# Hybrid encoder block: state sums moved into the output product of the SSM stage, paired sums merged

## The chip, the cores and the metric

One Trainium2 chip, one of its cores. The metric is the device time of one execution in microseconds (us). Engines are named as in the profile: PE (TensorE, matrix products; PEld its weight loads), DVE (VectorE), ACT (ScalarE), POOL (GpSimd), SP (SyncE, which here only issues DMAs). Each engine runs its own list of instructions in order; semaphores tie them together.

## The reference, cut to what matters

The kernel computes one encoder block over 2048 positions plus 16 learned meta tokens: an RMS norm, an input projection, a convolution group and a state-space group side by side, an output projection, a feed-forward part, and a final norm. The change lies in the state-space group (SSM, 32 groups of 16 channels, 64 complex states, two directions):

```
dt = jnp.exp(log_dt)[:, None];  lam_bar = jnp.exp(lam * dt)
b_bar = ((lam_bar - 1.0) / lam)[..., None] * b_mat
bu = jnp.einsum('gph,blgh->blgp', b_bar, u)            # input into the states
_, states = lax.associative_scan(op, (lam_bar, bu))    # x[l] = lam_bar * x[l-1] + bu[l], complex
return jnp.einsum('ghp,blgp->blgh', c_mat, states).real
```

The forward and the backward direction are added, a skip term D*u is added, and a GELU and a gated unit follow. All arithmetic is fp32.

## The kernel before, in words

The sequence is cut into 16 interleaved parts, so that the scan has to run over 130 columns only, with a 16-step product in front of it and one behind. Two groups of the 32 form a *block*, b = 0 to 15. The states of both directions lie on the 128 partitions (64 each).

For each block there is a preparation, `ssm_prep(b)`, and a run, `ssm_run(b)`. The preparation loads the block's packed parameters (tile `pkb`, two buffers), and forms complex outer products with `outer` (three products and two sums each, into `k1` and the result): `pb` (transposed on PE as `tr_wb`, copied to `wb`) and `pc` (three buffers) on DVE, and the table of phasors `tab`, cosine and sine, on POOL. A small product `k` of `pc` and `bk` (L701, L706) is sent to DRAM by ACT and read back by SP as the matrix `mt`.

The run loads `u`, multiplies it on PE with `wb` (the product called `v` at L737, into one PSUM buffer, not to be confused with the other tile called `v`, which is the convolution group's projection at L158 to L160), and then, on DVE: `r1`, `r2` (the product turned by the table: times cosine, times sine), `zi` (two sums, one real, one imaginary), two scans `zo` (one for each direction, with real decays `rh`), `s1`, `s2` (turned back: times cosine, times sine) and `st` (two sums). PE then forms the output product `y`: for each of four pieces two matmuls of `mt` with `u` (L770) and two of `pc` with `st` (L773), all summed in PSUM. ACT copies it out and sends it to DRAM. `r1`, `r2`, `zi`, `rh`, `zo` have one buffer each; `s1` and `s2` reuse those of `r1` and `r2`.

The scheduler of the language puts the instructions of all engines into one fixed order each, by priorities and its own costs. It places into the gaps on PE the projections of the convolution group and of the later `u` parts (tiles `u`, `g`, `v` at L158 to L160, 128x512 matmuls in groups of three). They are called *fillers* here: they do not depend on the SSM blocks, and those that do not stand between the blocks stand behind the last one. After the blocks come the gated unit, the convolution, the output projection and the feed-forward part, whose order in the program is untouched by the change: on every engine the lists are the same from the gated unit on.

The loop that drives the blocks is the lower one in the code: run b, then prepare b + 3.

Of the kernel before, what the change touches and what calls it, by code (L numbers as in the profile page):

```python
# [18 lines left out]
P = 128  # L19
# [3 lines left out]
H = 16  # L23
# [14 lines left out]
def hymba_kernel(ctx, tc, x, meta, norm_mix_g, w_in, conv_w, conv_b, conv_ln_g, conv_ln_b,  # L38
# [123 lines left out]
    with ExitStack() as es2:  # L162
# [181 lines left out]
        with (tc.tile_pool(name="pp", bufs=1, reuse_waits="tile") as PP,  # L344
# [133 lines left out]
            def ssm_params():  # L478
# [111 lines left out]
                for v in (bb, cc, phb):  # L590
                    sub(v[:, 2], v[:, 1], v[:, 0])
                    add(v[:, 3], v[:, 0], v[:, 1])
# [40 lines left out]
        with (tc.tile_pool(name="pb", bufs=1, reuse_waits="tile") as PB,  # L633
# [14 lines left out]
            def ssm_prep(b):  # L648
# [11 lines left out]
                def outer(o_re, o_im, a, b4, la, lb, on=V):  # L660
# [9 lines left out]
                    tt(o_re, k1, o_re, ALU.subtract)  # L670
                    tt(o_im, k1, o_im, ALU.add)
# [9 lines left out]
                outer(pb[:, :, 0], pb[:, :, 1], lpv, bb, minor(H), major(16))  # L681
# [10 lines left out]
                outer(pc[:, :, 0], pc[:, :, 1], lpc, cc, major(H), minor(16))  # L692
# [24 lines left out]
                for g in range(2):  # L717
                    for half in range(2):
                        SP.dma_start(mt[:, g, half, :],
                                     dap(gdr[b], (g * H + half * 8) * 34 * H + H, [[34 * H, 8], [H, 16], [1, 256]]))  # L720

                tab = tb_([P, 2, 2, 10, 13], f"tab{b}", tag="tab", bufs=3)
                outer(tab[:, 0], tab[:, 1], pha, phb, major(13), minor(10), GP)
                prep[b] = (wb, pc, mt, tab)

            def ssm_run(b):
# [15 lines left out]
                sinb = tabf[:, 1].unsqueeze(2).broadcast_to([P, 2, 2, W])  # L742
# [4 lines left out]
                mul(r2, psv, sinb)  # L747
                add(zi[:, :, 0, :], r1[:, :, 0, :], r2[:, :, 1, :])
                sub(zi[:, :, 1, :], r1[:, :, 1, :], r2[:, :, 0, :])
# [9 lines left out]
                s1 = tb_([P, 2, 2, W], f"s1_{b}", tag="r1")[:, :, :, 0:P]  # L759
                s2 = tb_([P, 2, 2, W], f"s2_{b}", tag="r2")[:, :, :, 0:P]  # L760
                mul(s1, zv, cosb[:, :, :, 2:W])
                mul(s2, zv, sinb[:, :, :, 2:W])
                st = tb_([P, 2, 2, P], f"st{b}", tag="st", bufs=2)
                sub(st[:, :, 0, :], s1[:, :, 0, :], s2[:, :, 1, :])
                add(st[:, :, 1, :], s1[:, :, 1, :], s2[:, :, 0, :])
                py = ks_ps(f"y{b}", [P, 2, 2, P])
                for g in range(2):
                    for ht in range(2):
# [3 lines left out]
                        for ri in range(2):  # L772
                            T.matmul(py[:, g, ht, :],  # L773
                                     pc[:, g, ri, 8 * ht:8 * ht + 8, :].rearrange("p i h -> p (i h)"),
                                     st[:, g, ri, :], start=False, stop=(ri == 1))
# [7 lines left out]
            for j in range(4):  # L783
                do_gv(0, j, by_block=(j == 3))
                if j < 3:
                    ssm_prep(j)
            z_block(2)
# [10 lines left out]
            for b in range(16):  # L798
                ssm_run(b)
                if b + 3 < 16:  # L800
                    ssm_prep(b + 3)
                if b in (1, 3):
# [445 lines left out]
```

## Time and profile before

| | |
|---|---|
| three runs | 2150.45, 2155.8, 2158.47 us; median 2155.8 |
| profiled execution | 2151.91 us, of it the span from first to last instruction 2150.1 us |
| PE clock granted, mean | 0.987 of full |
| share of the span busy | PE 95%, PEld 78%, DVE 72%, ACT 33%, POOL 8% |
| the SSM blocks | from the first block's product (234 us) to the last block's (461 us) |

The profile gives for each group of instructions the time that the engine was busy with it, the mean duration, and the idle time of the engine just before it with what ended that idle time. Durations of neighbouring instructions overlap a little, so that the distance from start to start is what one costs in a row. One fp32 matmul of 128 columns stands as two records in the trace: "x4" is two such matmuls. A matmul of the fillers is one record.

### The profile page before, as it was taken

The page shows a single profiled execution, that of the slowest core. Times are in us where ns is not written, and L with a number is a line of the kernel's source. Part 1 is how long each engine was busy: PE and PEld are TensorE (multiplying, and loading weights), DVE is VectorE, ACT ScalarE, POOL GpSimd, SP SyncE. Part 2 cuts the span into 40 slices and gives each one's busy share as a digit, 9 for nine tenths or more (in the row PEclk, how much of TensorE's full clock was granted, in tenths as well). Part 3 has the DMA queues.
Part 4 walks back from the last instruction along what each step waited for, and adds up shares of the span by engine and source line. Part 5 has one row for each costly group of instructions (what it writes and reads, how often), then busy time and mean ns, then how long its engine had stood idle before and what let it go on. Part 6 is the DMA issues. An engine that isn't in the chain of part 4 may idle for free.

```text
span 2150.1 us, 27315 instructions
## 1 busy us (share of the span) xinstructions
PE 2050.0 (95%) x10124; PEld 1682.7 (78%) x10124; DVE 1542.8 (72%) x2779; ACT 709.8 (33%) x1046; POOL 168.9 (8%) x257
## 2 busy tenths in 40 slices
PE   7989988899998999999999999997999999999997
PEld 5767777778886778888888888885888888888886
DVE  7866799965459697565568879778655656666767
ACT  5323222233232345444442313224444442212122
POOL 1031244600002010000000000001000000000000
PEclk9999999999999999999999999998999999999999
DMA  6245434334553674333353333325233325232322
GB/s 192 79 166 173 133 107 134 106 119 143 172 153 111 231 236 147 100 97 118 118 201 123 122 104 128 127 89 171 95 108 118 118 98 196 89 108 82 115 79 88
DMA packets 217485, 279.03 MB, mean 130 GB/s; under 512 B 31437, under 2 KB 164569, under 8 KB 216840
## 3 DMA queue, kind: packets, MB, share of 16 engines
q1 hardware_dynamic: 191720, 225.73, 34.1%
q10 hardware_dynamic: 23072, 43.10, 5.5%
q0 software_dynamic: 2560, 8.46, 1.0%
q8 instruction: 80, 1.31, 0.3%
q14 instruction: 53, 0.43, 0.1%
HBM read 195.39 MB, written 81.85 MB: 129 GB/s over the span
## 4 chain that ended last, share of the span: by engine, by line
PE 78%; DVE 12%; DMA 3%; issue 2%; ACT 1%; ACTq 0%; SPq 0%; DVEq 0%
PE f L158 10%; PE f L159 10%; PE f L160 10%; PE ps L1104 10%; PE ps L1103 10%; PE ps L1102 10%; PE wo L158 2%; PE wo L160 2%; PE wo L159 2%; PE cv L903 2%; DMA h<-hdr 1%; DVE zo L756 1%; DVE s L45 1%; DVE zo L755 1%; DVE r L45 1%
## 5 line engine op out<-in xcount | busy, mean ns | idle before, releaser
L45 DVE TENSOR_TENSOR acc<-acc,f 128x512 f32<-128x512 f32 x496 | 331.5, 684 | 142.7 <-PE f L160 142.1
L158 PE MATMUL f<-w,hid 128*128 128x512 f32 x1024 | 399.6, 390 | 1.8 <-DVE acc L45 1.8
L159 PE MATMUL f<-w,hid 128*128 128x512 f32 x1024 | 398.6, 389 | 0.0
L160 PE MATMUL f<-w,hid 128*128 128x512 f32 x1024 | 398.5, 389 | 0.0
L1104 PE MATMUL ps<-zx,w 128*128 128x512 f32 x896 | 352.9, 394 | 11.7 <-DVE w L142 11.7
L1102 PE MATMUL ps<-zx,w 128*128 128x512 f32 x896 | 353.3, 394 | 5.6 <-ACT w L141 5.6
L1103 PE MATMUL ps<-zx,w 128*128 128x512 f32 x896 | 353.2, 394 | 0.0
L158 PEld LDWEIGHTS f<-w,hid 128*128 128x128 f32 x1024 | 192.2, 188 | 43.2 <-DVE acc L45 3.7
L160 PEld LDWEIGHTS f<-w,hid 128*128 128x128 f32 x1024 | 192.2, 188 | 40.1
L159 PEld LDWEIGHTS f<-w,hid 128*128 128x128 f32 x1024 | 192.2, 188 | 39.5
L1104 PEld LDWEIGHTS ps<-zx,w 128*128 128x128 f32 x896 | 168.8, 188 | 51.1 <-DVE w L142 12.7
L1102 PEld LDWEIGHTS ps<-zx,w 128*128 128x128 f32 x896 | 169.1, 189 | 45.5 <-ACT w L141 6.7
L1103 PEld LDWEIGHTS ps<-zx,w 128*128 128x128 f32 x896 | 168.7, 188 | 38.4
L141 ACT CAST hid<-rawh 128x1024 fp32r<-128x1024 f32 x64 | 67.3, 1052 | 359.4 <-PE f L160 351.7
L142 DVE TENSOR_TENSOR w<-sm,w 128x512 fp32r<-128x512 f32 x128 | 87.7, 689 | 65.9 <-ACT w L141 65.9
L141 ACT CAST w<-sm 128x512 fp32r<-128x512 f32 x128 | 78.7, 618 | 163.0 <-PE ps L1104 141.5
L141 ACT CAST w<-r 128x512 fp32r<-128x512 f32 x96 | 58.8, 616 | 130.3 <-PE ps L1104 129.7
L141 ACT CAST w<-raww 128x1024 fp32r<-128x1024 f32 x64 | 67.3, 1052 | 91.5 <-DMA raww<-in_w_ff_dram 91.5
L142 DVE TENSOR_TENSOR hid<-rawh,hid 128x1024 fp32r<-128x1024 f32 x64 | 78.2, 1221 | 15.7 <-ACT hid L141 15.7
L142 DVE TENSOR_TENSOR w<-raww,w 128x1024 fp32r<-128x1024 f32 x64 | 78.0, 1219 | 8.9 <-ACT w L141 8.9
L45 DVE TENSOR_TENSOR hh<-c,ps 128x512 f32<-128x512 f32 x64 | 44.0, 687 | 47.5 <-PE ps L1104 46.2
L45 DVE TENSOR_TENSOR xo<-xo,wo 128x512 f32<-128x512 f32 x64 | 43.8, 685 | 31.9 <-PE wo L160 31.2
(302 smaller groups left out, 3385.7 us busy)
## 6 DMA issues: line engine op xcount, KB each, us to landing
r<-in_w_ff_dram SPq DMA_DIRECT2D x64, 512.0 KB
fdr<-hh ACTq DMA_DIRECT2D x64, 512.0 KB
rawh<-fdr SPq DMA_DIRECT2D x64, 512.0 KB
raww<-in_w_ff_dram SPq DMA_DIRECT2D x64, 512.0 KB
h<-hdr SPq DMA_DIRECT2D x32, 512.0 KB
x<-in_x_dram SPq DMA_DIRECT2D x16, 512.0 KB
mt<-gdr SPq DMA_DIRECT2D x64, 128.0 KB
xo<-in_x_dram SPq DMA_DIRECT2D x16, 512.0 KB
```

The lines of the kernel that those rows point to most:

```text
L45: return V.tensor_tensor(out=o, in0=a, in1=b, op=op)
L141: S.copy(out=hi, in_=src)
L142: on.tensor_tensor(lo, src, hi.bitcast(F32), ALU.subtract)
L158: T.matmul(ps, lh, rh, start=first, stop=False)
L159: T.matmul(ps, lh, rl, start=False, stop=False)
L160: T.matmul(ps, ll, rh, start=False, stop=last)
L755: V.tensor_tensor_scan(zo[0:64, 2:4 * W + 2], f(rh)[0:64, :], f(zi)[0:64, :], 0.0, ALU.mult, ALU.add)
L756: V.tensor_tensor_scan(zo[64:128, 0:4 * W][:, ::-1], f(rh)[64:128, ::-1], f(zi)[64:128, ::-1], 0.0, ALU.mult, ALU.add)
L903: T.matmul(ps[:, i], u8[:, i, 2 - m:2 - m + P], cb[:, 4 * (q % 2) + i, :, ts(m, 16)], start=(m == 0), stop=(m == 2))
L1102: T.matmul(ps[q], w[q][:, 0, k], z[:, 0, k, :], start=(k == 0), stop=False)
L1103: T.matmul(ps[q], w[q][:, 0, k], z[:, 1, k, :], start=False, stop=False)
L1104: T.matmul(ps[q], w[q][:, 1, k], z[:, 0, k, :], start=False, stop=(k == 3))
```

## The change

Three things are changed, all in the SSM stage.

The sums `st` are gone. The output product is linear, so PE multiplies `pc` with `s1` and with `s2` (the imaginary part of one against the real of the other) and sums in PSUM. For this the table gets a third plane, minus sine, made by ACT from the sine plane, so that `s2` carries its sign. `s1` now has its own two buffers (those of the former `st`); `s2` stays in the single buffer of `r2`, and is now read by PE until the end of the block's output product.

The two sums of `zi` become one instruction over 520 elements, which reads `r2` with its real and imaginary halves exchanged. The two last sums of every `outer` become one instruction over 1024 elements on DVE (520 on POOL), which reads `k1` twice; the sign for it is put into the parameters once, at the start of the kernel.

The table of block b + 2 is made after run b and preparation b + 3 (`ssm_tab`), into two buffers instead of three, so that the parameters `pkb` of a block are needed until its table is done.

In counts, per block: DVE has 2 instructions fewer for `st`, 1 for `zi`, 2 for the outer products; PE has 16 matmuls of `pc` in the place of 8 (the matmuls with `mt` and `u` stay at 8); POOL has one instruction fewer, ACT one more. Between the first block's product and the last block's output product the list of PE holds 338 fillers before and 303 now; the other 35 stand right behind the last block.

```diff
--- before.py
+++ after.py
@@ -589,7 +589,7 @@
                 sub(ai, t4[2], t4[3])
                 for v in (bb, cc, phb):
                     sub(v[:, 2], v[:, 1], v[:, 0])
-                    add(v[:, 3], v[:, 0], v[:, 1])
+                    stt(v[:, 3], v[:, 0], -1.0, v[:, 1], ALU.mult, ALU.subtract)
                 for v in (lpv, lpc, pha):
                     add(v[:, 2], v[:, 0], v[:, 1])
                 for i in range(4):
@@ -657,7 +657,7 @@
                 bb, cc, lpv, lpc = pv(0, 4, H), pv(128, 4, H), pv(256, 3, 16), pv(352, 3, 16)
                 pha, phb = pv(448, 3, 10), pv(508, 4, 13)
 
-                def outer(o_re, o_im, a, b4, la, lb, on=V):
+                def outer(o, o_re, o_im, a, b4, la, lb, on=V):
 
                     n = tuple(o_re.shape[2:])
                     q = "k1" if on is V else "k1g"
@@ -667,8 +667,9 @@
                     tt(k1, la(a[:, 2]), lb(b4[:, 0]), ALU.mult)
                     tt(o_im, la(a[:, 0]), lb(b4[:, 2]), ALU.mult)
                     tt(o_re, la(a[:, 1]), lb(b4[:, 3]), ALU.mult)
-                    tt(o_re, k1, o_re, ALU.subtract)
-                    tt(o_im, k1, o_im, ALU.add)
+                    k1 = k1.rearrange("p g x y -> p g (x y)")
+                    k1 = k1.unsqueeze(2).broadcast_to(list(o.shape)) if on is V else k1.unsqueeze(1).broadcast_to(list(o.shape))
+                    tt(o, k1, o, ALU.add)
 
                 def major(n):
                     return lambda v: v.unsqueeze(3).broadcast_to([P, 2, v.shape[2], n])
@@ -678,7 +679,7 @@
 
 
                 pb = tb_([P, 2, 2, H, 16], f"pb{b}", tag="pb")
-                outer(pb[:, :, 0], pb[:, :, 1], lpv, bb, minor(H), major(16))
+                outer(pb.rearrange("p g r x y -> p g r (x y)"), pb[:, :, 0], pb[:, :, 1], lpv, bb, minor(H), major(16))
                 wb = tb_([P, 2, 2, 2, P], f"wb{b}", tag="wb", bufs=3)
                 for g in range(2):
                     ps = tr_ps(f"tr_wb{b}_{g}", [P, 2, 2, P])
@@ -689,7 +690,7 @@
                     S.copy(out=wb[:, g], in_=ps)
 
                 pc = tb_([P, 2, 2, 16, H], f"pc{b}", tag="pc", bufs=3)
-                outer(pc[:, :, 0], pc[:, :, 1], lpc, cc, major(H), minor(16))
+                outer(pc.rearrange("p g r x y -> p g r (x y)"), pc[:, :, 0], pc[:, :, 1], lpc, cc, major(H), minor(16))
 
                 bk = tb_([P, 2, 2, H, 2], f"bk{b}", tag="bk")
                 GP.memset(bk, 0.0)
@@ -718,10 +719,19 @@
                     for half in range(2):
                         SP.dma_start(mt[:, g, half, :],
                                      dap(gdr[b], (g * H + half * 8) * 34 * H + H, [[34 * H, 8], [H, 16], [1, 256]]))
-
-                tab = tb_([P, 2, 2, 10, 13], f"tab{b}", tag="tab", bufs=3)
-                outer(tab[:, 0], tab[:, 1], pha, phb, major(13), minor(10), GP)
-                prep[b] = (wb, pc, mt, tab)
+                prep[b] = [wb, pc, mt, lambda: outer_tab(b, outer, pha, phb, major, minor)]
+
+            def outer_tab(b, outer, pha, phb, major, minor):
+
+                tab = tb_([P, 3, 2, 10, 13], f"tab{b}", tag="tab", bufs=2)
+                outer(tab[:, 0:2].rearrange("p r g x y -> p r g (x y)"), tab[:, 0], tab[:, 1], pha, phb, major(13),
+                      minor(10), GP)
+                S.mul(out=tab[:, 2], in_=tab[:, 1], mul=-1.0)
+                return tab
+
+            def ssm_tab(b):
+                if b < 16:
+                    prep[b][3] = prep[b][3]()
 
             def ssm_run(b):
                 g0 = 2 * b
@@ -739,14 +749,13 @@
                 psv = ps[:, :, 0:2 * W].rearrange("p g (r m) -> p g r m", r=2)
                 tabf = tab.rearrange("p r g a b -> p r g (a b)")
                 cosb = tabf[:, 0].unsqueeze(2).broadcast_to([P, 2, 2, W])
-                sinb = tabf[:, 1].unsqueeze(2).broadcast_to([P, 2, 2, W])
+                sin2 = tabf[:, 1:3].rearrange("p r g m -> p g r m")
                 r1 = tb_([P, 2, 2, W], f"r1_{b}", tag="r1")
                 r2 = tb_([P, 2, 2, W], f"r2_{b}", tag="r2")
                 zi = tb_([P, 2, 2, W], f"zi{b}", tag="zi")
                 mul(r1, psv, cosb)
-                mul(r2, psv, sinb)
-                add(zi[:, :, 0, :], r1[:, :, 0, :], r2[:, :, 1, :])
-                sub(zi[:, :, 1, :], r1[:, :, 1, :], r2[:, :, 0, :])
+                mul(r2, psv, sin2)
+                sub(zi, r1, r2[:, :, ::-1, :])
                 rh = tb_([P, 2, 2, W], f"rh{b}", tag="rh")
                 for g in range(2):
                     S.mul(out=rh[:, g], in_=mask.unsqueeze(1).broadcast_to([P, 2, W]), mul=rho[:, g0 + g:g0 + g + 1])
@@ -756,13 +765,10 @@
                 V.tensor_tensor_scan(zo[64:128, 0:4 * W][:, ::-1], f(rh)[64:128, ::-1], f(zi)[64:128, ::-1], 0.0,
                                      ALU.mult, ALU.add)
                 zv = zo[:, 0:4 * W].rearrange("p (g r m) -> p g r m", g=2, r=2)[:, :, :, 2:W]
-                s1 = tb_([P, 2, 2, W], f"s1_{b}", tag="r1")[:, :, :, 0:P]
+                s1 = tb_([P, 2, 2, P], f"s1_{b}", tag="st", bufs=2)
                 s2 = tb_([P, 2, 2, W], f"s2_{b}", tag="r2")[:, :, :, 0:P]
                 mul(s1, zv, cosb[:, :, :, 2:W])
-                mul(s2, zv, sinb[:, :, :, 2:W])
-                st = tb_([P, 2, 2, P], f"st{b}", tag="st", bufs=2)
-                sub(st[:, :, 0, :], s1[:, :, 0, :], s2[:, :, 1, :])
-                add(st[:, :, 1, :], s1[:, :, 1, :], s2[:, :, 0, :])
+                mul(s2, zv, sin2[:, :, :, 2:W])
                 py = ks_ps(f"y{b}", [P, 2, 2, P])
                 for g in range(2):
                     for ht in range(2):
@@ -770,9 +776,10 @@
                             T.matmul(py[:, g, ht, :], mt[:, g, half, ts(ht, P)], u[:, g, half, 1:1 + P],
                                      start=(half == 0), stop=False)
                         for ri in range(2):
-                            T.matmul(py[:, g, ht, :],
-                                     pc[:, g, ri, 8 * ht:8 * ht + 8, :].rearrange("p i h -> p (i h)"),
-                                     st[:, g, ri, :], start=False, stop=(ri == 1))
+                            for q, r in ((s1, ri), (s2, 1 - ri)):
+                                T.matmul(py[:, g, ht, :],
+                                         pc[:, g, ri, 8 * ht:8 * ht + 8, :].rearrange("p i h -> p (i h)"),
+                                         q[:, g, r, :], start=False, stop=(ri == 1 and q is s2))
                 ys = tb_([P, 2, 2, P], f"ys{b}", tag="ys", bufs=2)
                 S.copy(out=ys, in_=py)
                 for g in range(2):
@@ -784,6 +791,8 @@
                 do_gv(0, j, by_block=(j == 3))
                 if j < 3:
                     ssm_prep(j)
+                if j in (1, 2):
+                    ssm_tab(j - 1)
             z_block(2)
             z_tiles(2, 0, 2)
             z_tiles(2, 2, 2)
@@ -799,6 +808,7 @@
                 ssm_run(b)
                 if b + 3 < 16:
                     ssm_prep(b + 3)
+                ssm_tab(b + 2)
                 if b in (1, 3):
                     do_u(1, 2 + b // 2)
             for j in range(4):
```

The list of DVE behind `s2` of block 7, before: the sums `st7`, the last sums of `pb` of block 10, the next block's `r1` and `r2`, and then `pc` of block 10, whose buffer was that of `pc` of block 7, so that it waits for PE's output product `y7`.

```order
L45 TENSOR_TENSOR s2_7_3338<-zo7_3334,tab7_3068 128x4x128
L45 TENSOR_TENSOR stv0_2_4278<-v0_2_4253,sg0_2_4224 128x4x128 [waits DMASW7_49,PE_49]
L45 TENSOR_TENSOR st7_3341<-s1_7_3337,s2_7_3338 128x2x128 [waits DVE_49]
L45 TENSOR_TENSOR st7_3341<-s1_7_3337,s2_7_3338 128x2x128
L670 TENSOR_TENSOR pb10_3369<-k1_10_3370,pb10_3369 128x2x256
L671 TENSOR_TENSOR pb10_3369<-k1_10_3370,pb10_3369 128x2x256
L45 TENSOR_TENSOR r1_8_3443<-v8_3434,tab8_3187 128x520 [waits DVE_49,Pool_49]
L667 TENSOR_TENSOR k1_10_3390<-pkb10_3367 128x512 [waits DVE_49]
L45 TENSOR_TENSOR r2_8_3444<-v8_3434,tab8_3187 128x520
L45 TENSOR_TENSOR zi8_3445<-r1_8_3443,r2_8_3444 128x2x130 [waits DVE_49]
L668 TENSOR_TENSOR pc10_3389<-pkb10_3367 128x2x256 [waits PE_49]
```

The same place now.

```order
L45 TENSOR_TENSOR s2_7_3338<-zo7_3334,tab7_3186 128x4x128
L668 TENSOR_TENSOR pb10_3374<-pkb10_3372 128x2x256
L669 TENSOR_TENSOR pb10_3374<-pkb10_3372 128x2x256
L45 TENSOR_TENSOR r1_8_3446<-v8_3437,tab8_3307 128x520 [waits Pool_49]
L672 TENSOR_TENSOR pb10_3374<-k1_10_3375,pb10_3374 128x1024 [waits DVE_49]
L667 TENSOR_TENSOR k1_10_3394<-pkb10_3372 128x512 [waits DVE_49]
L668 TENSOR_TENSOR pc10_3393<-pkb10_3372 128x2x256 [waits PE_49]
L669 TENSOR_TENSOR pc10_3393<-pkb10_3372 128x2x256
L45 TENSOR_TENSOR r2_8_3447<-v8_3437,tab8_3307 128x520
L672 TENSOR_TENSOR pc10_3393<-k1_10_3394,pc10_3393 128x1024 [waits DVE_49]
L45 TENSOR_TENSOR zi8_3448<-r1_8_3446,r2_8_3447 128x520 [waits DVE_49]
```

`r2` of block 8 now stands behind the first instruction that waits for `y7`, and before it between `s2` and that wait are five instructions. In the others it is one (blocks 1 and 3), two (0 and 5), four (2, 4, 6, 9, 10 and 12), five (11) or six (8); in blocks 13 and 14 no preparation is left, the wait is that of the next `r2`, and none and one stand before it.

The list of PE at the output product of block 7 before, from its first matmul with `st` on (the product's first two matmuls of `mt` and `u` stand ahead of the fillers in front).

```order
L773 MATMUL y7_3344<-st7_3341,pc7_3032 128x128 [waits DVE_49] x2
L770 MATMUL y7_3344<-u7_3313,mt7_3063 128x128 x2
L773 MATMUL y7_3344<-st7_3341,pc7_3032 128x128 x2
L770 MATMUL y7_3344<-u7_3313,mt7_3063 128x128 [waits DMAHW3_49]
L770 MATMUL y7_3344<-u7_3313,mt7_3063 128x128 [waits DMAHW4_49]
L773 MATMUL y7_3344<-st7_3341,pc7_3032 128x128 x2
L770 MATMUL y7_3344<-u7_3313,mt7_3063 128x128 x2
L773 MATMUL y7_3344<-st7_3341,pc7_3032 128x128 x2
```

The same place now, from the first matmul that needs `s2` on; the first with `s1` stands two fillers ahead.

```order
L780 MATMUL y7_3341<-s2_7_3338,pc7_3030 128x128 [waits DVE_49]
L780 MATMUL y7_3341<-s1_7_3337,pc7_3030 128x128
L780 MATMUL y7_3341<-s2_7_3338,pc7_3030 128x128
L776 MATMUL y7_3341<-u7_3314,mt7_3060 128x128 x2
L780 MATMUL y7_3341<-s1_7_3337,pc7_3030 128x128
L780 MATMUL y7_3341<-s2_7_3338,pc7_3030 128x128
L780 MATMUL y7_3341<-s1_7_3337,pc7_3030 128x128
L780 MATMUL y7_3341<-s2_7_3338,pc7_3030 128x128
L776 MATMUL y7_3341<-u7_3314,mt7_3060 128x128
L776 MATMUL y7_3341<-u7_3314,mt7_3060 128x128 [waits DMAHW3_49]
L780 MATMUL y7_3341<-s1_7_3337,pc7_3030 128x128
L780 MATMUL y7_3341<-s2_7_3338,pc7_3030 128x128
```

Behind the matmul that needs the last of DVE's results there were 14 of the product's 16 before (12 behind the second sum, where `st` comes in two); now there are 21 of 24 behind the first that needs `s2` and with it 22.

## Rows read from the trace of the kernel before

**Rows 1.** Page, part 1: busy us, share of the span, instructions of each engine.

```profile
PE 2050.0 (95%) x10124; PEld 1682.7 (78%) x10124; DVE 1542.8 (72%) x2779; ACT 709.8 (33%) x1046; POOL 168.9 (8%) x257
```

**Rows 2.** Windows, SSM blocks and after: PE, PEld, DVE, ACT, POOL busy, clock, DMA.

```profile
234.00:461.00 227.00, 199.34 (x1513) 171.12 (x1514) 213.23 (x321) 52.69 (x101) 95.69 (x122) 0.98 0.39 111
461.00:640.00 179.00, 178.62 (x975) 152.84 (x974) 97.10 (x189) 55.97 (x86) 5.34 (x7) 1.00 0.52 159
```

**Rows 3.** Waits, 234 to 461 us: total, times, longest.

```profile
PE y L773 <- DVE st L45: 12.4, 16, 1.3
...
PE v L737 <- DMA u<-udr: 4.9, 5, 1.8
```

**Rows 4.** Groups by shape, DVE, 234 to 461 us: busy, mean ns, idle before.

```profile
L667 DVE TENSOR_TENSOR k<-pkb 128x512 f32<-128x512 f32 x24 | 23.3, 972 | 0.1
...
L45 DVE TENSOR_TENSOR st<-s,s 128x256 f32<-128x256 f32 x32 | 19.3, 633 | 0.2
L45 DVE TENSOR_TENSOR zi<-r,r 128x260 f32<-128x260 f32 x32 | 14.5, 479 | 0.4
...
L668 DVE TENSOR_TENSOR pc<-pkb 128x512 f32<-128x512 f32 x13 | 9.6, 740 | 0.5 <-PE y L773 0.4
```

**Rows 5.** Timeline, DVE: start, duration; the first scan of blocks 2, 4, 9, 13.

```profile
269.29 1.23 DVE L755 TENSOR_TENSOR_SCAN zo<-rh,zi 64x520 f32<-64x520 f32 x1
...
300.09 1.22 DVE L755 TENSOR_TENSOR_SCAN zo<-rh,zi 64x520 f32<-64x520 f32 x1
...
375.35 1.22 DVE L755 TENSOR_TENSOR_SCAN zo<-rh,zi 64x520 f32<-64x520 f32 x1
...
383.59 0.68 DVE L667 TENSOR_TENSOR k<-pkb 128x512 f32<-128x512 f32 x1
384.19 0.68 DVE L45 TENSOR_TENSOR r<-v,tab 128x520 f32<-128x520 f32 x1
384.91 0.77 DVE L45 TENSOR_TENSOR zi<-r,r 128x260 f32<-128x260 f32 x2
...
422.38 1.29 DVE L45 TENSOR_TENSOR s<-zo,tab 128x512 f32<-128x512 f32 x2
...
427.49 1.21 DVE L142 TENSOR_TENSOR w_v<-raw_v,w_v 128x1024 fp32r<-128x1024 f32 x1
428.62 0.68 DVE L671 TENSOR_TENSOR pb<-k,pb 128x512 f32<-128x512 f32 x1
...
434.25 0.35 DVE L62 SCALAR_TENSOR_TENSOR g<-ident,dcol,k 16x16 f32<-16x16 f32 x2
434.53 1.22 DVE L755 TENSOR_TENSOR_SCAN zo<-rh,zi 64x520 f32<-64x520 f32 x1
```

**Rows 6.** Timeline, PE: start, duration, idle time before.

```profile
350.38 0.49 PE L773 MATMUL y<-st,pc 128*128 128x128 f32 x2 [0.29 <-DVE st L45]
...
394.33 0.61 PE L770 MATMUL y<-u,mt 128*128 128x128 f32 x4
394.78 0.61 PE L773 MATMUL y<-st,pc 128*128 128x128 f32 x4
...
398.35 0.39 PE L159 MATMUL v<-zl,w_v 128*128 128x512 f32 x1
398.58 0.40 PE L160 MATMUL v<-zh,w_v 128*128 128x512 f32 x1
...
400.71 1.13 PE L737 MATMUL v<-u,wb 128*128 128x130 f32 x8 [1.26 <-DMA u<-udr]
...
460.75 0.61 PE L773 MATMUL y<-st,pc 128*128 128x128 f32 x4
```

**Rows 7.** Timeline, SP's queue: the issue of `u` of block 11.

```profile
396.76 0.36 SPq L731 DMA_DIRECT2D u<-udr  x1
```

**Rows 8.** Timeline, POOL, block 0's preparation (first and last of twelve).

```profile
131.38 0.70 POOL L696 COPY bk<-pkb 64x64 f32<-64x64 f32 x1 [18.41 <-DMA pkb<-kdr]
...
138.35 0.72 POOL L670 TENSOR_TENSOR tab<-k1g,tab 128x260 f32<-128x260 f32 x1
```

**Rows 9.** Timeline, DVE, at the same place and in block 6.

```profile
132.54 7.08 DVE L669 TENSOR_TENSOR pb<-pkb 128x512 f32<-128x512 f32 x1
...
318.89 2.70 DVE L667 TENSOR_TENSOR k<-pkb 128x512 f32<-128x512 f32 x1
```

## The prediction

> **What bounds the kernel now.** I read the page's shares first [rows 1]: PE is busy 95% of the span, DVE 72%. A PE that is nearly full makes an edit that gives PE more work suspect, but the share is a mean over stages. So the windows come next [rows 2]. From 234 to 461 us, the SSM blocks, PE is busy 199.3 of 227 us and DVE 213.2; from 461 on PE is busy 178.6 of 179, without a gap. The reader is to see two regimes: in the blocks both engines have a little room and neither is full; behind them PE alone is the limit. Two rules follow. What the change does to the time is (a) the shift of the end of the last block's output product, and (b) all PE work that is pushed behind it, at full price.
>
> Third, the waits inside the blocks [rows 3]: PE waits 12.4 us for `st`, 16 times, once in each block, and 4.9 us for `u`. DVE waits for PE's output product only 0.4 us, at `pc` [rows 4]. So the blocks hang on a chain that goes mostly through DVE: turn, scan, turn back, sum, then PE. Last, the timelines give the pitch. From the first scan of one block to that of another [rows 5], blocks 2 to 4 take 30.8 us (15.4 each), 4 to 9 take 75.26 (15.05 each), 9 to 13 take 59.18 (14.8 each).
>
> **The change part by part.**
>
> *DVE gets shorter.* By start-to-start distances [rows 5] an operation over 512 or 520 elements costs 0.60, over 1024 elements 1.13, two of 256 or 260 some 0.68 (the pair of `zi` at 384.91 is 0.77 with overlap). Removed: `st`, 16 x 0.68 = 10.9. Merged: `zi`, 16 x (0.68 - 0.61) = 1.1; the last two sums of `pb` and `pc`, 25 x (1.20 - 1.13) = 1.75. Together 13.7. Beside this, `st` ran at a mean of 633 ns where an undisturbed one takes about 410 (my estimate, 0.34 and the overlap), another 7 us, if the disturbance is not merely passed on [rows 4].
>
> *PE gets longer.* A 128-column fp32 matmul costs 0.445 / 2 = 0.2225 (394.33 to 394.78 holds two) [rows 6]. Eight more per block: 128 x 0.2225 = 28.5 us. By busy time PE has 227 - 199.3 = 27.7 us free in the blocks [rows 2]; so the added work fits only if it falls exactly into the gaps. The order of the program does not try it: 35 fillers that stood between the blocks stand behind them now. At 0.233 each (398.35 to 398.58) [rows 6] they cost 8.2 us there, where nothing hides them. They also relieve the blocks by 8.2, but a relief of PE in the blocks counts only where PE sets the pitch.
>
> The Trainium skill, "TensorE: Matmul & The Clock Gate", section "Back-to-back issue gap", gives about 81 ns for one matmul of 128 columns in a sustained stream; by it the 128 would be 10.4 us. The trace disagrees for these fp32 matmuls, 222 ns each [rows 6], and the measurement decides.
>
> *A new wait.* Before, PE's output product read `st`, which had two buffers, and `s2` was free as soon as `st` was formed. Now PE reads `s2` itself until the end of the product. Behind the first matmul that needs `s2` stand 21 more, so the product ends 0.29 (handover, the gap at 350.38) [rows 6] + 21 or 22 x 0.2225 = 4.7, together 5.0 us after `s2`. Two things on DVE must wait for that end: `pc` of block b + 3, which takes the buffer of `pc` of block b, and `r2` of block b + 1, in the one buffer of `s2`. Behind that waiting `pc` on DVE stand `r2`, `zi`, the scans of the next block: the whole chain. Before, the same `pc` waited only 12 matmuls, some 3.0 us behind the last sum, with 1.8 to 4.4 us of DVE work ahead of it, hence the 0.4 [rows 4]. Now what stands between `s2` and the wait is, priced as above: two to five instructions of 0.6 to 1.13, that is 1.2 us (block 0), 0.6 (1 and 3), 2.4 (2, 4), 2.95 (6, 9, 10, 12), up to 4.7 (8), 0 (13). It never reaches 5.0, so DVE waits in every block.
>
> The pitch after therefore is 5.0 plus the DVE work from the wait to the next `s2`. Steady blocks: `pc` 1.20, `r2` 0.61, last sum 1.13, `zi` 0.61, `k1` 0.60, two small products 0.28 (434.25 to 434.53), scans 2.46, one product of `pb` 0.60, `s1` and `s2` 1.20, in all 8.69 [rows 5]. 13.7 so; POOL's small copies beside DVE and the gate products and weight splits that now and then stand here bring about 0.65: 14.35 against 14.8, **-1.8** for the four of blocks 9 to 13. Blocks 4 to 9 have more splits (1.13 each) [rows 5]: 14.8 against 15.05, **-1.3**. The early blocks have more DVE work behind the wait: an odd one 5.0 + 9.2 = 14.2, an even one, with a split and the next `pb`, 17.2, and 0.8 for POOL's copies: 32.2 against 30.8, **+1.4** for blocks 2 to 4 and as much for 0 to 2. The tail, from `s2` of block 12 (423.67) to the end of the last product (461.36), is 37.7 before [rows 5, 6]; after, 12.5 (5.0 and the last preparation's part) + twice 9.9 (5.0 and `r2`, `zi`, scans, `s1`, `s2`, 4.88) + 5.0 = 37.3, **-0.4**. The sum in the blocks is -0.7. That is less than its terms are sure to, so I take 0; the ends are -10 (the 13.7 of DVE without `u`'s and the early blocks' price) and +17 (`u` uncovered, below).
>
> *The load of `u`* is released when the product's last matmul with `u` has run, four matmuls (0.9) before its end. From issue (396.76) to the first `v` (400.71) pass 3.95 [rows 6, 7], and only the transposes (0.79) and five fillers (1.17) stand ahead of `v`: PE idles about 1.3 a block. That lies beside DVE's chain (PE stood 12.4 / 16 = 0.8 a block waiting for `st` [rows 3], and will stand so for `s1`) and I cost it at nothing; without that cover it is up to 1.3 x 13 blocks = 17 us.
>
> *The table*, made later now, by POOL, with the sign plane by ACT: I cost it at nothing, since a block's table is not needed before `r1` two blocks on. What it does to DVE is the second rival. The start of the kernel keeps its two tables in a row, and with them the block of 7.08 us [rows 9]; no change there.
>
> **Sum.** 0 in the blocks + 8.2 for the spilled fillers: 2151.9 + 8.2 = 2160.1 for the profiled execution; the median of the runs stands 3.9 above that execution, so 2164.
>
> **Rivals.**
>
> *POOL holds DVE up behind `s2` (slower, more).* While POOL worked through twelve operations in a row (131.38 to 139.1) one DVE product took 7.08 us instead of 0.68, and another 2.70 in block 6 [rows 8, 9]. Now POOL starts the table just when `s2` is done, beside the DVE products of `pb`, which read two SBUF tiles. If POOL's four operations (three of 0.63, the distance in that row of twelve, and one of twice the elements, 1.3 by estimate: 3.2) lock DVE out, 2.95 becomes 6.15, past the 5.0: +1.2 in 13 blocks = +15.6, time 2180. For it: these rows; against it: `st`, beside POOL before, lost only 0.22 each on average [rows 4], and wherever less than 2 us stands ahead of the wait the lockout is hidden under it. The Trainium skill, "SBUF — State Buffer", section "Who interferes with whom", says that a DVE operation with two SBUF inputs contends with a GpSimd operation that reads SBUF, and that the first to issue keeps the other out altogether. By that rule this rival holds; rows 8 and 9 agree with it at two places, `st`'s mean agrees with it in part.
>
> *DVE's saving comes through (faster).* If the chain that sets the pitch has DVE time in it that the y wait now absorbs (POOL's disturbance falls into idle DVE), the blocks lose 13.7 and half of the 7, some 17: 17 - 8.2 = 9 faster, 2147. For it: DVE was the busier engine, 213 of 227 [rows 2]. Against it: 5.0 a block is longer than the DVE work ahead of the wait everywhere, and by busy time PE would have only 27.7 - 28.5 + 8.2 = 7.4 us of idle left to give [rows 2].
>
> *The change does nothing that shows.* Half of the new wait is covered, the blocks give 8 back and the fillers take 8: 2156.
>
> **How the numbers follow.** Forecast 0.56, within 2157 to 2171 by the price of the early blocks and the cover of `u`; POOL's lockout 0.17; faster 0.14; nothing 0.13. A difference under 0.5% (10.8 us: 2145.0 to 2166.6) can't be told from none. Faster takes the lower part of its case and the tail of "nothing", 0.13. Slower takes the lockout, 0.17, and 0.25 of the forecast, whose centre is 2.6 below the bound: 0.42. The rest, 0.45, is the same. The range reaches from 2143, just past the centre of the faster case, to 2184, past that of the lockout: the nearer halves of both are in, and about 2 in 10 is left out.
>
> **What would show it.** Right: no `st` row; a new wait of DVE, `pc` (and `r2` in the last two blocks) for PE `y`, of 20 to 35 us over blocks 0 to 14; 256 matmuls with `s1` and `s2` at 0.22; the last product ending near 461; 35 fillers right behind it and PE full from there. Wrong: that wait absent or under 10 us; the last product ending before 450 or after 470; DVE products of 2 us and more behind `s2`, in most blocks, which would speak for the lockout.

## The result

The changed kernel takes 2166.75 us (median of 13 runs, 2157.07 to 2171.31), the kernel before 2152.65 beside it: a ratio of 1.0059, with a 95% interval of 1.0044 to 1.0073. That is 12.7 us slower where 8.2 were forecast. The time lies in the range, on the edge between "no change" and "slower". Medians are of the fast executions; two that took far longer (2303.53 us of the kernel before, 4207.51 us of the kernel e6 below) are left out.

The profiled execution of the changed kernel is its shortest, 2157.07 us, with a mean granted clock of 0.992; the other twelve ran at 0.985 to 0.992. Its span is only 5.1 us longer than that of before, so where it differs must be read stretch by stretch. Windows, cut at the first output product, the end of the last one, and the gated unit. Before (columns: window, its length, busy time and instructions of PE, PEld, DVE, ACT, POOL, granted clock, DMA share, GB/s):

```profile
236.12:461.36 225.24, 197.81 (x1501) 169.59 (x1500) 212.34 (x319) 52.69 (x101) 95.47 (x120) 0.98 0.39 110
461.36:493.87 32.51, 32.51 (x141) 26.16 (x140) 17.36 (x23) 11.84 (x19) 4.80 (x6) 1.00 0.41 132
```

And after:

```profile
230.45:462.24 231.79, 214.22 (x1722) 187.84 (x1721) 187.33 (x247) 56.51 (x112) 77.23 (x113) 1.00 0.38 108
462.24:502.91 40.67, 40.67 (x176) 32.74 (x176) 17.93 (x24) 13.65 (x22) 4.51 (x6) 1.00 0.35 110
```

The blocks take 231.8 instead of 225.2 us, **+6.6**. The fillers behind them take 40.67 instead of 32.51, **+8.2**, with 176 instead of 141 instructions: the 35 spilled ones. Together +14.7.

Ahead of the blocks the change acts too: the first output product starts **5.7** us earlier, behind as many PE instructions (1190). Before, then after:

```profile
0.00:236.12 236.12, 206.47 (x1190) 162.14 (x1191) 162.79 (x492) 86.03 (x147) 37.46 (x98) 0.98 0.50 154
0.00:230.45 230.45, 205.04 (x1190) 160.85 (x1191) 156.93 (x483) 86.58 (x149) 32.68 (x90) 0.99 0.51 156
```

PE idles 25.4 us there instead of 29.7. One place of it: the DVE product of 7.08 us [rows 9] takes 2.54 now, and PE's wait behind it is 1.63 instead of 4.84 (DVE after, PE before, PE after):

```profile
133.60 2.54 DVE L669 TENSOR_TENSOR pb<-pkb 128x512 f32<-128x512 f32 x1
```

```profile
140.89 1.97 PE L687 MATMUL tr_wb<-ident,pb 128*128 128x128 f32 x8 [4.84 <-DVE pb L670]
```

```profile
139.49 1.09 PE L688 MATMUL tr_wb<-ident,pb 128*128 128x128 f32 x8 [1.63 <-DVE pb L672]
```

The early start does not look like chance: in the table below the eight kernels that make the table later, as the change does, start the blocks at 228.8 to 232.2 us, the four changed ones that make it in the preparation ("early table") at 233.6 to 236.2, and the two with the stage as before at 236.1 and 238.3. How the later table brings it about was not followed; the shorter product alone does not, since e5 has it too (2.52 us).

So up to the gated unit the change costs -5.67 + 6.55 + 8.16 = **9.0** us. From there to the end of the span pass 1652.3 instead of 1656.3 us, with code that the change does not touch. The medians lie 14.1 us apart (12.7 by the ratio); what lies above 9.0 is not shown by this execution.

What the changed kernel waits for inside the blocks (columns: who waits for whom, total us, times, longest), beside [rows 3]:

```profile
DVE pc L668 <- PE y L780: 15.1, 7, 4.4
DVE pb L668 <- DMA pkb<-kdr: 11.4, 3, 4.1
DVE r L45 <- PE y L780: 9.6, 2, 5.0
PE v L747 <- DMA u<-udr: 8.0, 7, 2.8
...
PE y L780 <- DVE s L45: 3.8, 6, 1.0
```

Of the 12.4 us that PE waited for `st`, 3.8 are left, for `s`. In exchange DVE, which had waited 0.4 for the product [rows 4], waits 24.7, in nine places. The product's group:

```profile
L780 PE MATMUL y<-s,pc 128*128 128x128 f32 x512 | 72.5, 279 | 3.9 <-DVE s L45 3.8
```

512 records are 256 matmuls, as foreseen; from start to start they cost what [rows 6] gives (four in 0.89 us, from 421.76 to 422.65).

The pitch, by the first scan of blocks 0, 2, 4, 9 and 13 in DVE's timeline (start, duration), to be laid beside [rows 5]:

```profile
232.73 1.23 DVE L764 TENSOR_TENSOR_SCAN zo<-rh,zi 64x520 f32<-64x520 f32 x1
...
264.34 1.22 DVE L764 TENSOR_TENSOR_SCAN zo<-rh,zi 64x520 f32<-64x520 f32 x1
...
297.30 1.22 DVE L764 TENSOR_TENSOR_SCAN zo<-rh,zi 64x520 f32<-64x520 f32 x1
...
371.55 1.22 DVE L764 TENSOR_TENSOR_SCAN zo<-rh,zi 64x520 f32<-64x520 f32 x1
...
429.28 1.23 DVE L764 TENSOR_TENSOR_SCAN zo<-rh,zi 64x520 f32<-64x520 f32 x1
```

Blocks 2 to 4 take 33.0 us (30.8 before), 4 to 9 74.25 (75.26), 9 to 13 57.7 (59.2): a pitch of 14.4 where 14.35 had been worked out. From the scan of 13 to the end of the last product pass 32.9 us, before 26.8. The loss sits at both ends; the middle gains.

### The profile page after: what moved, and what is told of

Same layout as the page of the kernel before. It is cut to its first block, busy times and chain, and to the rows that moved or that the text cites. A ratio compares the mean times of both kernels' runs of the same rounds, so it can differ in the third digit from the quotient of the medians.

```text
span 2155.2 us, 27754 instructions
## 1 busy us (share of the span) xinstructions
PE 2070.3 (96%) x10380; PEld 1704.5 (79%) x10380; DVE 1511.7 (70%) x2699; ACT 716.3 (33%) x1062; POOL 146.1 (7%) x241
## 4 chain that ended last, share of the span: by engine, by line
PE 81%; DVE 8%; DMA 4%; issue 1%; ACT 1%; ACTq 0%; POOL 0%; DVEq 0%; SPq 0%
PE f L158 10%; PE f L159 10%; PE f L160 10%; PE ps L1114 10%; PE ps L1113 10%; PE ps L1112 10%; PE y L780 2%; PE wo L158 2%; PE wo L160 2%; PE wo L159 2%; PE cv L913 2%; PE y L776 1%; DMA u<-udr 1%; DMA h<-hdr 1%; DMA pkb<-kdr 1%
## 5 line engine op out<-in xcount | busy, mean ns | idle before, releaser
L1114 PEld LDWEIGHTS ps<-zx,w 128*128 128x128 f32 x896 | 168.8, 188 | 51.1 <-DVE w L142 12.7
L780 PE MATMUL y<-s,pc 128*128 128x128 f32 x512 | 72.5, 279 | 3.9 <-DVE s L45 3.8
```

What stands on the lines that cost most here:

```text
L780: T.matmul(py[:, g, ht, :], pc[:, g, ri, 8 * ht:8 * ht + 8, :].rearrange("p i h -> p (i h)"), q[:, g, r, :], start=False, stop=(ri == 1 an ...
L1114: T.matmul(ps[q], w[q][:, 1, k], z[:, 0, k, :], start=False, stop=(k == 3))
```

## The experiments

Each was timed beside the kernel before. The other columns are from the one profiled execution of each, in us: the start of the blocks (first output product), L, the length of the blocks (to the end of the last output product), S, that of the fillers behind them, the gated unit, which begins at start + L + S, and PE's idle time in L. In S PE is never idle.

| kernel | median | ratio to before, 95% interval | start | L | S | gated unit | idle in L |
|---|---|---|---|---|---|---|---|
| before | 2152.65 to 2153.73 | 1 | 236.1 | 225.2 | 32.5 | 493.9 | 27.4 |
| the change | 2166.75 | 1.0059 [1.0044, 1.0073] | 230.5 | 231.8 | 40.7 | 502.9 | 17.6 |
| e1 s2 own buffer | 2178.15 | 1.0122 [1.0102, 1.0142] | 231.6 | 232.0 | 57.9 | 521.5 | 30.2 |
| e2 pc four buffers | 2178.94 | 1.0116 [1.0096, 1.0136] | 228.8 | 229.9 | 56.5 | 515.1 | 27.8 |
| e3 both | 2173.78 | 1.0093 [1.0073, 1.0113] | 229.1 | 220.4 | 62.6 | 512.1 | 25.7 |
| e4 sums formed again | 2165.99 | 1.0056 [1.0038, 1.0074] | 229.9 | 237.5 | 37.6 | 505.0 | 37.9 |
| e5 the same, early table | 2157.44 | 1.0021 [1.0012, 1.0031] | 236.2 | 229.0 | 34.4 | 499.6 | 30.4 |
| e6 the change, early table | 2168.01 | 1.0065 [1.0050, 1.0080] | 235.3 | 231.6 | 40.7 | 507.6 | 15.0 |
| e7 s2 own, early table | 2178.53 | 1.0119 [1.0103, 1.0135] | 235.7 | 231.0 | 57.7 | 524.3 | 29.7 |
| e8 half product | 2160.87 | 1.0029 [1.0017, 1.0041] | 230.2 | 224.2 | 47.4 | 501.8 | 38.1 |
| e9 u three buffers | 2158.68 | 1.0032 [1.0020, 1.0044] | 232.1 | 230.9 | 40.0 | 503.0 | 15.4 |
| e10 before, u three buffers | 2153.03 | 1.0002 [0.9992, 1.0012] | 238.3 | 221.1 | 37.9 | 497.2 | 28.1 |
| e11 half product, early table | 2165.25 | 1.0053 [1.0041, 1.0065] | 233.6 | 223.5 | 46.3 | 503.4 | 34.6 |
| e12 s2 own, u three buffers | 2176.83 | 1.0106 [1.0091, 1.0121] | 232.2 | 219.7 | 67.0 | 519.0 | 26.6 |

To make room for a third or fourth buffer, e2, e3, e5 to e7 and e9 to e12 leave `ys` and `gst` one buffer each instead of two. What this costs alone was not tried; e6 and e10, which have it, stay at the times of the change and of the kernel before.

**Taking the wait away.** Three kernels free DVE from PE's product.

e1:

```diff
-                s1 = tb_([P, 2, 2, P], f"s1_{b}", tag="st", bufs=2)
-                s2 = tb_([P, 2, 2, W], f"s2_{b}", tag="r2")[:, :, :, 0:P]
+                s1 = tb_([P, 2, 2, P], f"s1_{b}", tag="st", bufs=1)
+                s2 = tb_([P, 2, 2, P], f"s2_{b}", tag="s2", bufs=1)
```

> s2 gets a buffer of its own (s1 gives one of its two for it, the space is the same), so r2 of the next block no longer waits for PE's product; pc still does, but the order now puts it behind the scans, some 6 us after s2. Theory W (the new wait of DVE on PE's product costs the time, 5 us a block of which DVE works only part): the pitch falls from 14.5 to about 12.3 us, the sum of DVE's work in a block; the order leaves 229 fillers in the blocks instead of 303, so 74 x 0.233 = 17 us come back behind them; 15 x 2.2 - 17 = 16 us less than the changed kernel, about 2151, as fast as before. Rival P (what costs is the 28.5 us of PE work alone, the wait only decides where PE idles): PE gains nothing, 2166 within 4 us, all that the blocks give up comes back as fillers.

e2:

```diff
-                pc = tb_([P, 2, 2, 16, H], f"pc{b}", tag="pc", bufs=3)
+                pc = tb_([P, 2, 2, 16, H], f"pc{b}", tag="pc", bufs=4)
```

> pc gets a fourth buffer (ys and gst give one of two each), so pc no longer waits for PE's product of three blocks before; r2 still waits for that of the block before. Theory W: the wait moves to r2, with the preparation's DVE work in front of it (pc, pb) now covering most of the 5 us; only blocks 13 and 14, where no preparation is left, wait in full. 68 fillers fewer in the blocks (16 us). Some 10 to 14 us less than the changed kernel, 2153 to 2157. Rival P: 2166 within 4 us.

e3, both edits:

> Both: s2 with its own buffer and pc with four; nothing on DVE waits for the product of the block before. Theory W: not much beyond the better of the two alone, since one of them already lets DVE work through; 2148 to 2156; the DVE waits on PE's product in the blocks fall from 25 us to under 4. Rival P: 2166 within 4 us, with the idle time of DVE replaced by waits on other results of PE (v, y).

All three came out slower than the changed kernel. Theory W fell, and rival P, which foresaw 2166 within 4 us, missed too. The waits of e1 in the blocks (228 to 470 us) show where the time went:

```profile
PE v L747 <- DMA u<-udr: 14.4, 7, 5.1
DVE r L45 <- PE v L747: 12.9, 3, 7.0
DVE g L62 <- ACT gst L710: 11.0, 6, 2.8
DVE pc L668 <- PE y L780: 7.9, 4, 3.6
PE k L702 <- DVE pc L672: 6.9, 4, 2.0
```

The wait for the product is down to 7.9, and others have taken its place. One instance, in SP's queue and then in PE's timeline:

```profile
425.09 2.45 SPq L720 DMA_DIRECT2D mt<-gdr  x4
427.64 0.40 SPq L741 DMA_DIRECT2D u<-udr  x1
```

```profile
432.84 3.81 PE L747 MATMUL v<-u,wb 128*128 128x130 f32 x16 [5.06 <-DMA u<-udr]
```

`u` stands behind the four loads of `mt` in SP's queue, PE idles 5.06 us, and then its granted clock is 0.50 from 432.84 to 436.20, while it works on this `v` (the lower of its two levels, 1.2 instead of 2.4 GHz); over the blocks it is 0.96 instead of 1.00. So L stayed at 232. But the order was laid out for shorter blocks: it leaves 229 fillers in them instead of 303, and the others are paid for behind, 57.9 us against 40.7:

```profile
231.59:463.56 231.97, 201.80 (x1648) 181.97 (x1647) 192.91 (x243) 52.10 (x109) 89.47 (x107) 0.96 0.35 102
463.56:521.49 57.93, 57.93 (x249) 46.75 (x249) 22.33 (x28) 16.35 (x25) 6.60 (x12) 1.00 0.34 104
```

In e2 the first wait of a preparation became one for its parameters:

```profile
DVE k L667 <- DMA pkb<-kdr: 31.2, 11, 3.6
```

In e3 the wait for the product went, as W said (1.1 us left), and the blocks got 11.4 us shorter (220.4); but S took back 21.9. In these blocks it is PE that waits for DVE again:

```profile
PE y L780 <- DVE s L45: 17.6, 12, 2.3
```

**Undoing parts.** e4 forms the sums again (`add(st, s1, s2[:, :, ::-1, :])`, and PE multiplies `pc` with `st`, 8 matmuls a block); merges and later table stay.

> The folding of the sums alone is undone: st is formed again on DVE (with the third plane that takes one sum over 512 elements instead of two over 256), and PE multiplies pc with st, 8 matmuls a block; the merged sums and the later table stay. Both theories expect a time below before: the merges save DVE 16 x 0.07 (st) + 1.1 (zi) + 1.75 (outer) = 4 us and cost nothing on PE, so 2148 to 2152 if DVE sets the pitch. Rival O (the later table and the load order behind it cost by themselves): above 2158.

It takes as long as the change, as rival O, the later table, had it (above 2158). POOL's last step on the parameters, then SP's queue, then PE:

```profile
341.85 1.78 POOL L669 TENSOR_TENSOR tab<-pkb 128x260 f32<-128x260 f32 x1
```

```profile
343.67 0.33 SPq L651 DMA_DIRECT2D pkb<-kdr  x1
344.12 2.44 SPq L720 DMA_DIRECT2D mt<-gdr  x4
346.67 0.40 SPq L741 DMA_DIRECT2D u<-udr  x1
```

```profile
351.56 3.81 PE L747 MATMUL v<-u,wb 128*128 128x130 f32 x16 [5.66 <-DMA u<-udr]
```

The next `pkb` is issued as soon as the table has read the last one; `mt` and `u` stand behind it, and PE idles 5.66 us. e5 puts the table back into the preparation:

```diff
-                prep[b] = [wb, pc, mt, lambda: outer_tab(b, outer, pha, phb, major, minor)]
+                prep[b] = [wb, pc, mt, outer_tab(b, outer, pha, phb, major, minor)]
-                tab = tb_([P, 3, 2, 10, 13], f"tab{b}", tag="tab", bufs=2)
+                tab = tb_([P, 3, 2, 10, 13], f"tab{b}", tag="tab", bufs=3)
```

> As the kernel with the sums formed again on DVE, and the table made in the preparation, where it was before, with three buffers (ys and gst give one of two each). What is left of the change is the merges alone. Theory Q (the later table holds the parameters pkb longer, and on SP's one queue the loads of mt and u stand behind the load of the next pkb, so u comes late: PE waited 20.9 us for u and its clock fell in eight stretches in the last run): that goes, and with 4 us of DVE saved the time is 2147 to 2151, 15 less than with the later table. Rival M (the merged instructions are what costs): it stays at 2160 to 2168.

It gives back 0.35% of the 0.56%, which speaks for Q (PE's wait for `u` in the blocks fell from 20.4 to 11.4 us), but its time lies between the ranges of both theories: the merges alone do not bring their 4 us, they are 0.21% slower than before. e6 is the same edit on the changed kernel.

> The changed kernel with the table made in the preparation, as before, in three buffers. Folding and merges stay. Theory Q alone (the table is the whole loss): 2150 to 2155. Theory F (in the changed kernel itself u stands ahead of mt in SP's queue and PE waited only 8 us for it, so the loss is the folding's: 28.5 us more on PE and 5 us of waiting a block): 2160 to 2168, near the changed kernel's 2166.

F holds, at the upper end of its range: with the folding in, the table's place is worth nothing that can be measured (the intervals of e6 and of the change overlap). From e5 to e6, both with the early table and timed side by side, the folding costs **0.44%**, with intervals that do not overlap. This pair is the cleanest measure of it, and their profiles say where it lies: S grew by 6.3 us (176 instead of 148 instructions), L by 2.6, and the start came 0.9 earlier. Most of the folding's price is spilled fillers. e7 adds the buffer of e1 to e6.

> Folding and merges, s2 in its own buffer, and the table in the preparation. The first run with s2 in its own buffer was slower (2178) while PE waited 14.4 us for u. Theory W and Q together: with u in time the wait's price comes out, 8 to 15 us less than with the wait (the run beside this one), near 2150. Theory P (PE's 28.5 us are the loss whatever DVE waits for): no gain on the run beside this one, both 2160 to 2168.

As slow as e1, and above both ranges: PE waited 17.7 us for `u`, so the late `u` of e1 was not the table's doing.

**The product at half its price.** e8 leaves the eight matmuls with `s2` away; e11 is e8 with the early table.

```diff
-                            for q, r in ((s1, ri), (s2, 1 - ri)):
+                            for q, r in ((s1, ri),):
```

> The changed kernel without the eight matmuls of s2 in each block (the output lacks that part of the product), so PE has the work of before and nothing waits for s2; the later table stays. Theory P or F: 28.5 us of PE work less and the wait down to 3 us: 2138 to 2146. Theory Q: u comes late as with the sums formed again, 2155 to 2166.

> Half of the product as in the run before (the eight matmuls of s2 in each block are left out, the output lacks them), and the table made in the preparation as before. What is left is the folding's saving on DVE without its price on PE. Theory A: PE's work is that of before, 214.8, so only idle time counts; the early table brings it down from 42.9 by some 8 to 12, as it did with the sums formed again; 2148 to 2153. If DVE's saving were worth its 13.7 us on the path: 2138 to 2142.

e8 stays 0.29% above before, e11 0.53%, although PE has no more work than before and DVE lacks `st`. Theories F and P expected e8 some 10 us below before and fell; Q, with a late `u`, had its range right. For e11 theory A and the other figure both missed: the early table did not help. L is 224.2 and 223.5, hardly less than 225.2, with 47.4 and 46.3 us of fillers behind. PE idles more than before, 38.1 and 34.6 us, at a granted clock of 0.95 in the blocks, and the first of its waits is for `u` in e8 and nearly so in e11:

```profile
PE v L747 <- DMA u<-udr: 13.5, 5, 6.7
```

```profile
PE v L747 <- DMA u<-udr: 9.1, 5, 2.5
```

So DVE's saving, without PE's price, did not come through here, and the 28.5 us of PE work alone do not explain the loss.

**Loading u earlier.** e9 gives `u` three buffers in the changed kernel (`ys` and `gst` one each), e10 in the kernel before, e12 in e1.

```diff
-                u = tb_([P, 2, 2, W], f"u{b}", tag="u", bufs=2)
+                u = tb_([P, 2, 2, W], f"u{b}", tag="u", bufs=3)
```

> The changed kernel with three buffers for u (ys and gst give one of two each), so that u of block b + 2 can be loaded a block earlier. Theory A (formed after the runs so far: from the first output product to the gated unit the time is PE's work, 243.6 us now and 214.8 before, plus PE's idle and slowed time in the blocks; the folding adds 28.7 of work and can only give back idle time, of which the changed kernel has 20.8, 9.8 of it ahead of v): the idle time ahead of v falls from 9.8 to under 3, the time by 6 to 8 us, to 2158 to 2161. Rival W2 (DVE's wait sets the pitch, u is hidden beside it): 2164 to 2169, the idle time turns up ahead of y instead.

> The kernel before with the same three buffers for u. Theory A: its 5.5 us of idle time ahead of v go, with some of the 8.4 of slowed clock; 23 fillers fewer in the blocks must be paid by shorter blocks; 2146 to 2151, faster than both kernels. Rival W2: 2152 to 2157, no change.

> s2 with its own buffer and u with three: the wait of DVE for the product is gone from r2, and u comes in time. The order leaves 190 fillers in the blocks. Theory A: the 17.3 us idle ahead of v go, but 39 fillers more stand behind (9 us), and what the blocks gain is idle time given back, so 2160 to 2170, under the 2178 of the run with s2's buffer alone, still above before. Theory W (the wait is the loss, and u hid the gain of taking it away): 2145 to 2153.

e9 came out as A said (2158 to 2161): 8 us faster than the change by the medians, 6 by the ratios to the kernel before beside each, whose intervals touch at 1.0044. PE's waits in it:

```profile
PE y L780 <- DVE s L45: 7.2, 11, 1.0
...
PE v L747 <- DMA u<-udr: 0.5, 1, 0.5
```

The wait for `u` went from 8.0 to 0.5, that for `s` rose from 3.8 to 7.2. The profiled executions do not show a gain: L + S is 1.6 us less, the start 1.7 later. The one of the change was its shortest; where the time between the medians lies is not shown. e10 is no faster than before, against A and as W2 had it: L fell by 4.2, S rose by 5.4. e12 lies above both its ranges; `u` is in time in it, and the wait turned up at the product `k`:

```profile
PE k L702 <- DVE pc L672: 16.0, 10, 3.3
...
PE y L780 <- DVE s L45: 8.0, 10, 1.5
...
PE v L747 <- DMA u<-udr: 0.6, 1, 0.6
```

L is the shortest of all, 219.7, and S the longest, 67.0.

## Why the prediction was right, and which term was mis-sized

**The sum, and the luck in it.** Up to the gated unit 0 + 8.2 us were forecast, and the profile has 9.0. The fillers came as priced. But the end of the last product "near 461" came true, at 462.24, only because two terms cancel that were both put at nothing: the blocks are 6.6 us longer, and they start 5.7 us earlier, where the prediction had "no change there" for the start of the kernel. That the forecast of the whole came so near is in this part luck.

**The spilled fillers.** 8.2 us, measured 8.16. Exact, since nothing hides work behind the last block: PE is busy 40.67 of 40.67 us there.

**The blocks.** Priced at 0, measured +6.6; this, with the start, is the term that was mis-sized. Its middle was right: -1.0 for blocks 4 to 9 (-1.3 foreseen), -1.4 for 9 to 13 (-1.8). Blocks 0 to 2 came to +0.8 (+1.4), 2 to 4 to +2.2 (+1.4). The tail failed. From the end of `s2` of block 12 it was to take 37.3 us, and took 41.8 (420.40 to 462.24); the prediction's pieces also overlapped there, since that end lies before the scan of 13. Without overlap, from that scan on, the tail lost 6.1 against before. DVE's timeline in it, from the first instruction behind `s2` of block 12 on:

```profile
420.40 0.68 DVE L669 TENSOR_TENSOR pb<-pkb 128x512 f32<-128x512 f32 x1
...
432.07 0.70 DVE L45 TENSOR_TENSOR r<-v,tab 128x520 f32<-128x520 f32 x1
432.69 0.68 DVE L45 TENSOR_TENSOR s<-zo,tab 128x512 f32<-128x512 f32 x1
433.29 0.68 DVE L45 TENSOR_TENSOR stv<-v,sg 128x512 f32<-128x512 f32 x1
433.89 0.68 DVE L45 TENSOR_TENSOR s<-zo,tab 128x512 f32<-128x512 f32 x1
439.62 0.70 DVE L45 TENSOR_TENSOR r<-v,tab 128x520 f32<-128x520 f32 x1 [5.05 <-PE y L780]
...
450.14 0.70 DVE L45 TENSOR_TENSOR r<-v,tab 128x520 f32<-128x520 f32 x1 [4.56 <-PE y L780]
...
452.84 0.66 DVE L45 TENSOR_TENSOR stv<-v,sg 128x512 f32<-128x512 f32 x1
453.53 1.24 DVE L765 TENSOR_TENSOR_SCAN zo<-rh,zi 64x520 f32<-64x520 f32 x1
454.80 1.23 DVE L142 TENSOR_TENSOR w_v<-raw_v,w_v 128x1024 fp32r<-128x1024 f32 x1
455.94 1.29 DVE L45 TENSOR_TENSOR s<-zo,tab 128x512 f32<-128x512 f32 x2
```

The two waits have the size that was foreseen, 5.0 (the second is 4.56 behind a product of 0.69). Of the 4.5 us too few, 3.0 are instructions left out that stand on the path: `r1` of block 14 (0.62) and a gate product (0.60) ahead of block 13's `s1` and `s2`, a gate product (0.69) between the last two scans, and a weight split (1.14) ahead of the last `s1`. They could have been counted in the order. The other 1.5 are small gaps.

**The wait.** Its sum of 24.7 us lies within the 20 to 35. But "in every block" was wrong: it shows in nine of fifteen. In three early blocks DVE waited for `pkb` just ahead of it (11.4 us); in the steady ones POOL's table lay beside what stands ahead of the wait, as here:

```profile
378.58 1.65 DVE L672 TENSOR_TENSOR pb<-k,pb 128x1024 f32<-128x1024 f32 x1
380.26 1.67 DVE L667 TENSOR_TENSOR k<-pkb 128x512 f32<-128x512 f32 x1
382.50 0.69 DVE L668 TENSOR_TENSOR pc<-pkb 128x512 f32<-128x512 f32 x1 [0.56 <-PE y L780]
```

with POOL at the same time:

```profile
378.51 0.63 POOL L669 TENSOR_TENSOR tab<-pkb 128x260 f32<-128x260 f32 x1
379.22 2.16 POOL L672 TENSOR_TENSOR tab<-k1g,tab 128x520 f32<-128x520 f32 x1
```

The two DVE instructions lose about 0.5 and 1.0 us, the wait behind them is 0.56. So the rival of POOL's lockout had the mechanism and lost by its size: with 1.5 instead of 3.2 us the 2.95 ahead of the wait become some 4.45, still under the 5.0 that cover them. The rows fit engines that take turns: DVE's sum ends as if begun at 379.14, when POOL's product ends, and DVE's `k` ends 0.55 us after POOL's sum (381.38); each waits for one instruction of the other, not for all four, as the product of 2.70 us at 318.89 [rows 9] did. The longest DVE instruction of a preparation in the blocks is one of 2.30 us; the other lengthened ones take 1.65 to 1.67.

**The load of `u`** was put at nothing, under the cover of DVE's chain. PE waited 8.0 us for it; with `u` in time (e9) L fell by 0.9 only, and the wait for `s` rose by 3.4. The profiles agree with the cover; the medians of e9, 6 to 8 us lower, leave it open.

**Taking the wait away does not give its price back.** It sets the pitch of the steady blocks, and the pitch was computed from it to 0.1 us (with 0.65 of it an estimate). Taken away, it gives the time only to the next waits, `u` through SP's queue, then `k` or `s`, and to fillers behind the blocks. The "faster" rival lost with it: DVE's saving did not come through even where PE had no more to do (e8, e11). The "does nothing" rival lost in the blocks, which gave no 8 us back but took 6.6 more.

**What the runs do show** is a balance on PE. S is work, L is work and PE's idle time. The change makes PE busy for 24.6 us more in L + S (28.5 were priced; the granted clock in the blocks is 1.00 instead of 0.98) and its idle time 9.9 less, together the +14.7. The kernels that take DVE's wait away move fillers out of the blocks, and PE is idle again, 26 to 30 us instead of 17.6. So L fell by less than S rose: 11.4 against 21.9 in e3 and 12.1 against 26.4 in e12, each against the change; 1.8 against 13.8 in e11 and 4.2 against 5.4 in e10, each against before. Of these reliefs only e9, which left the order nearly as it was, lost nothing that way. **Open** is what holds L near 220: in e3 PE waits for DVE's `s`, in e12 for `k` and `s`. Every edit here also moves fillers, so no run shows a relief with the order held: whether e3 or e10 with the 338 fillers kept between the blocks would be faster than before was not tried. No kernel run here is faster than the kernel before.

## What to carry to other kernels

When an engine off the limit is relieved, add up the limiting engine's work over the stage and what is left behind it: a stage that is laid out as shorter gets less filler work, and if it does not get as short as it was laid out, the change loses on both counts. A buffer that a second engine now reads is a new wait, and its price is computed from the order (instructions behind the wait's source, less those ahead of the waiting one); what its removal is worth is not that price but the distance to the next wait. Look at the in-order DMA queue for it: the load that matters stands behind loads that wait for something else.

## What was not expected

Moving the table later cost 0.35% with the sums on DVE (e5 to e4) and nothing with the sums on PE (e6 to the change). In both pairs the blocks start earlier (by 6.3 and 4.9 us) and PE waits longer for `u` (20.4 instead of 11.4 us, and 8.0 instead of 2.8); that the balance of the two makes the difference is argued, not shown.

The time of an execution of the changed kernel follows its mean granted clock: 2157.07 us at 0.992 and 2171.31 at 0.985, about 2 us for each 0.001, which is what 0.001 of 2155 us comes to. In the kernel before the tie is looser. One profiled execution can therefore differ from the median by as much as the change itself, here by 9.7 us; only a comparison by stretches, with the clock of each, was of use.
